# Softmax divisors moved from the probabilities to the attention outputs, with GpSimd issuing and multiplying

## The chip, the cores and the metric

The program runs on one core of a Trainium2 chip. The metric is the device time of one execution in microseconds; lower is better. The engines of the core work side by side, each through its own instructions in a fixed order: TensorE (PE, with its weight loads PEld), VectorE (DVE), ScalarE (ACT), GpSimd (POOL) and SyncE (SP, which here only issues transfers). An instruction that has to wait holds up everything behind it on its engine, and SP's queue of transfers behaves in the same way.

## The reference

One layer of a hybrid encoder on x[1024, 1024] in float32: RMSNorm, one input projection, three token mixers side by side (pooling, gated linear attention, forgetting attention), an output projection with residual, RMSNorm, a SwiGLU feed-forward part, a last RMSNorm. The change touches only the forgetting attention, eight heads of 64 channels:

```python
s = einsum('bhqd,bhkd->bhqk', qb, kh) + Fb[..., None] - F[:, :, None, :]
s = where(kpos[None, :] <= qpos[:, None], s, -inf)
p = softmax(s, axis=-1)                 # exp(s - max) / sum over the row
return einsum('bhqk,bhkd->bhqd', p, vh)
```

The division by a row's sum may stand on the probabilities or, since the product with V is linear, on the output of the row.

## The kernel before

Heads are worked in four pairs p = 0 to 3; a = 0 or 1 is the head in the pair. A head's 1024 queries are cut into eight blocks of 128; an item (a, m) holds two neighbouring blocks, qb = 2m and 2m + 1. `fox_item` does one item: for each block PE makes the scores (lines 575 to 578), DVE adds the forget term and finds the row's extreme (580), ACT takes the exponential and sums the row (584). Then DVE inverts the two sums (587), POOL multiplies the first block's probabilities by it (590) and DVE the second's (592). PE turns the probabilities over (601), ACT and DVE split each turned tile into a high and a low float32r half (603, 604), PE multiplies them with V (615), and ACT and DVE add the two halves of the output (618, 621). The output is laid with channels on partitions and queries along the free axis, so that in it a row's divisor lies along the free axis.

The outputs of pairs 0 to 2 gather in a tile Y and go through `keep_mix` (272 to 276): an ACT and a DVE pass, and two transfers to DRAM. Pair 3 writes its halves straight into `last_mix` (623 to 625).

The other work of this part of the program is projections that need no attention: Q and K of the next pair (`zq`, `zk`), V of pairs 2 and 3 (`psv`, from weights `wfv`), and, beside pairs 2 and 3, the output projection over channel tiles 0 to 3 (`pxa`) and then 4 to 7 (`pxb`, line 144, with weights `wo4` to `wo7`, each in a high and a low half). A scheduler of the framework orders each engine's instructions when the program is built; so an edit moves instructions far from its own lines.

Buffers come from numbered slots. Two rings matter. Ring `wr` has two slots; every raw projection weight passes through it: it is loaded by SP, split by ACT (high half, 118) and POOL (low half, 119), and only then may the slot's next user be written:

```python
RINGS = {"p": 6, "pp": 3, "fb": 2, "wr": 2, "w": 4}
def load_w(src, name, n=1024, eng=None):
    raw, (hi, lo) = R(f"{name}r", tag="wr"), (R(f"{name}{h}", F32R, tag="w") for h in "hl")
```

After pair 3 the slots of the rings `wr`, `w`, `p`, `pp` and `fb` join the common pool of slots (711, 712), in which the next tile takes the slot that was freed longest ago. Ring `fb` (two slots) holds the forget terms of the pair's two heads, broadcast by SP (631).

Of the kernel before, what the change touches and what calls it, by code (L numbers as in the profile page):

```python
# [18 lines left out]
P = 128  # L19
# [12 lines left out]
def tile_hybrid_block(ctx: ExitStack, tc, x, w_fv, w_gv, w_zt, w_o, w_gu, w_down, ln, w_pool, w_a3, chans, b_f, consts, out):  # L32
    nc = tc.nc
    ACT, DVE, POOL, PE, SP = nc.scalar, nc.vector, nc.gpsimd, nc.tensor, nc.sync
# [4 lines left out]
    dpool = ctx.enter_context(tc.tile_pool(name="dp", bufs=1, space=bass.MemoryType.DRAM))  # L39
# [10 lines left out]
    def G(name, dtype=F32):  # L50
        i = idle.pop(0)
        t_ = big.tile([P, 1024], dtype, tag=f"g{i}", name=name)
        where[name] = i
        return t_

    def free(*names):
        for n in names:
            idle.append(where.pop(n))

    def R(name, dtype=F32, tag="p"):  # L60

# [50 lines left out]
    def PS(tag, name):  # L112
        return pst.tile([P, 512], F32, tag=tag, name=name, bufs=BANKS[tag])
# [22 lines left out]
    def half(name, dtype=F32):  # L136
        return rng.tile([P, 512], dtype, tag="tmp", name=name, bufs=2)
# [25 lines left out]
    def names_T(name):  # L163
        return [f"{name}{k}_{c}_{h}" for k in range(4) for c in range(2) for h in range(2)]
# [127 lines left out]
    last_mix = []  # L292
# [253 lines left out]
                    POOL.tensor_copy(t_[a][own[1 - a], csl], f(t_[a][own[a], csl]))  # L546
        return Q, K, KL

    def fox_item(p, a, m, ops, fb, V, Y):

        Q, K, KL = (t_[a] for t_ in ops)
        nm = f"{p}_{a}_{m}"
        rows = slice(64 * a, 64 * a + 64)
        Pb, Ws = [], []
        l, rl = S(f"l{nm}", 2), S(f"rl{nm}", 2)
        for i in range(2):
            qb = 2 * m + i
            W = P * (qb + 1)
            nh = 1 if W <= 512 else 2
            w = W // nh  # L560
            qs = slice(qb * P, (qb + 1) * P)
            mn = S(f"mn{nm}_{i}")
            if m >= 2:
                pb = R(f"pb{nm}_{i}")
            elif i == 0:
                pb2 = R(f"pb{nm}")
                pb = pb2[:, 0:512]
            else:
                pb = pb2[:, 512:1024]
            top = 3.0e38  # L570
            for h in range(nh):
                s = PS("s", f"s{nm}_{i}_{h}")
                ks = slice(h * w, (h + 1) * w)
                last = h == nh - 1
                PE.matmul(s[:, 0:w], Q[:, qs], K[:, ks], start=True, stop=False)  # L575
                PE.matmul(s[:, 0:w], Q[:, qs], KL[:, ks], start=False, stop=not last)  # L576
                if last:
                    PE.matmul(s[:, w - P:w], identr, maskr, start=False, stop=True)
                t_ = mn if last else S(f"mw{nm}_{i}")
                DVE.tensor_tensor_reduce(out=pb[:, ks], in0=s[:, 0:w], in1=fb[:, ks], scale=1.0, scalar=top,  # L580
                                         op0=ALU.add, op1=ALU.min, accum_out=t_)
                top = t_[:, 0:1]

            ACT.activation(pb[:, 0:W], pb[:, 0:W], AF.Exp, bias=mn[:, 0:1], scale=-1.0, accum_out=l[:, i:i + 1])
            Pb.append(pb)
            Ws.append(W)
        DVE.reciprocal(rl, l)  # L587
        for i, (pb, W) in enumerate(zip(Pb, Ws)):
            if i == 0:
                POOL.tensor_tensor(out=pb[:, 0:W], in0=pb[:, 0:W], in1=rl[:, 0:1].broadcast_to([P, W]), op=ALU.mult)  # L590
            else:
                DVE.tensor_scalar(out=pb[:, 0:W], in0=pb[:, 0:W], scalar1=rl[:, 1:2], scalar2=None, op0=ALU.mult)
        o = PS("o", f"o{nm}")
        for n in range(m + 1):
            pt = PS("pt", f"pt{nm}_{n}")
            pp = R(f"pp{nm}_{n}", F32R, tag="pp")
            cut = P if n == m else 0
            for b in range(2):
                for i in range(b if cut else 0, 2):
                    o0 = 256 * b + P * i - cut * b  # L600
                    PE.transpose(pt[:, o0:o0 + P], Pb[i][:, (2 * n + b) * P:(2 * n + b + 1) * P], ident)  # L601
            w = 512 - cut
            ACT.activation(pp[:, 0:w], pt[:, 0:w], AF.Copy)  # L603
            DVE.tensor_tensor(out=pp[:, 512:512 + w], in0=pt[:, 0:w], in1=f(pp[:, 0:w]), op=ALU.subtract)  # L604
            for b in range(2):
                kb = 2 * n + b
                o0 = cut * b
                v_ = V[p % 2][kb // 4][:, kb % 4, a]
                ph = pp[:, 256 * b:512 - o0] if b else pp[:, 0:256]
                pl = pp[:, 768:1024 - o0] if b else pp[:, 512:768]  # L610
                both = (o[:, o0:256], v_.rearrange("p s e -> p (s e)"), ph)
                high = (o[0:64, o0:256], v_[:, 0], pl)
                last = kb == 2 * m + 1
                for n_, args in enumerate((high, both) if last else (both, high)):
                    PE.matmul(*args, start=(kb == 0 and n_ == 0), stop=(last and n_ == 1))  # L615
        tmp = half(f"ot{nm}")
        ot, oy = tmp[0:64, 0:256], tmp[:, 256:512]
        ACT.activation(ot, o[64:128, 0:256], AF.Copy)
        if p < 3:
            oy = Y[:, m * 256:(m + 1) * 256]  # L620
        DVE.tensor_tensor(out=oy[rows], in0=o[0:64, 0:256], in1=ot, op=ALU.add)
        if p == 3:
            hi, lo = (last_mix[m // 2][rows, h, (m % 2) * 256:(m % 2 + 1) * 256] for h in range(2))
            ACT.activation(hi, oy[rows], AF.Copy)
            POOL.tensor_tensor(out=lo, in0=oy[rows], in1=f(hi), op=ALU.subtract)

    def fox_attend(p, ops, V, Y):
        fbs = []
        for a in range(2):
            fb = R(f"fb{p}_{a}", tag="fb")  # L630
            SP.dma_start(fb, Fd[2 * p + a:2 * p + a + 1, :].broadcast_to([P, T]))
            fbs.append(fb)
        for a, m in ([(a, m) for a in range(2) for m in range(4)] if p < 3 else [(a, m) for m in (1, 0, 3, 2) for a in range(2)]):
            fox_item(p, a, m, ops, fbs[a], V, Y)


    x3d = [dpool.tile([P, D], F32, name=f"x3d{tb}") for tb in range(NT)]
# [36 lines left out]
    V = fox_values(0, (B.within(1), o_[0][:1], o_[0][1:], o_[1][:1], o_[1][1:] + B.turned(0), B.turned(1), (), ()))  # L674
    for k in range(8):
        keep_wo(k)
    ops = fox_qk(0)
    free("gv0", "gv1", "attb0", "attb1")
    for p in range(4):
        if p == 3:  # L680
            last_mix += [G(f"mix7_{g}", F32R).rearrange("p (h t) -> p h t", h=2) for g in range(2)]
        Y = G(f"y{p}") if p < 3 else None
        fox_attend(p, ops, V, Y)
# [12 lines left out]


    ws = [fetch_wo(k) for k in range(4)]
# [284 lines left out]
    sums = {}  # L983
# [139 lines left out]
```

## Time and profile before

| | |
|---|---|
| median of three runs | 1176.26 us (1174.48 to 1177.74) |
| the profiled execution | 1175.42 us, with a span of 1173.7 us from first to last instruction, so 1.7 us lie around the span |
| granted TensorE clock, mean | 0.992 |
| PE, DVE, ACT, POOL busy | 97%, 71%, 46%, 29% of the span |
| the attention pairs with their projections | about 226 to 478 us |
| output projection and second norm, up to the feed-forward part | to about 545 us |

The page's PE row counts a pipelined matmul from its start to its modelled end, so that PE reads as full at nearly any density; where it matters the pitch from one start to the next is used. Names such as `psv` or `wo5l` are the program's tiles with numbers left out.

### The profile page before, as it was taken

To read this page: it belongs to the slowest core of one execution; us is meant where nothing else is said; L and a number is where in the kernel's file an instruction comes from. 1 tells how busy PE (TensorE), PEld (TensorE's weight loads), DVE (VectorE), ACT (ScalarE), POOL (GpSimd) and SP (SyncE) were. 2 spreads that over 40 slices of the span, in tenths; PEclk is the share of its full clock that TensorE was granted. 3 is DMA by queue.
4 is the path that set the end of the run, shared out by engine and by line. 5 is a ranking of instruction groups with operands and counts; after the bars stand their busy time and mean duration, and the time that the engine had idled before them with its cause. 6 is when DMAs were issued, how large, how long until landed. Compare 5 with 4: busy or idle time off the path is not lost.

```text
span 1173.7 us, 15953 instructions
## 1 busy us (share of the span) xinstructions
PE 1136.0 (97%) x5928; PEld 958.5 (82%) x5928; DVE 828.2 (71%) x1365; ACT 536.0 (46%) x970; POOL 340.4 (29%) x260
## 2 busy tenths in 40 slices
PE   6999998999999999998999999999999999999996
PEld 5877878889978888886888888888888888888875
DVE  6697364387746866579997767767686685876686
ACT  6454233466654644456453433444344344334345
POOL 2231123343322413210302221022201370660784
PEclk9999999999999999999999999999999999999999
DMA  7121184411203734431323332242314688333233
GB/s 250 37 73 52 59 295 174 176 39 35 91 18 126 305 132 159 173 112 46 117 86 129 101 115 88 101 134 82 135 54 152 224 322 293 103 95 102 86 112 143
DMA packets 57692, 150.45 MB, mean 128 GB/s; under 512 B 5080, under 2 KB 5512, under 8 KB 57616
## 3 DMA queue, kind: packets, MB, share of 16 engines
q1 hardware_dynamic: 57184, 147.87, 36.5%
q0 software_dynamic: 432, 1.57, 0.4%
q8 instruction: 46, 0.75, 0.3%
q14 instruction: 30, 0.25, 0.1%
HBM read 105.09 MB, written 44.34 MB: 127 GB/s over the span
## 4 chain that ended last, share of the span: by engine, by line
PE 76%; DVE 4%; DMA 1%; issue 1%; POOL 1%; ACT 1%; SPq 0%; POOLq 0%; DVEq 0%; ACTq 0%
PE m L774 36%; PE d L1030 15%; PE pxa L144 4%; PE pxb L144 3%; PE o L615 3%; PE pt L601 2%; PE psv L152 2%; PE s L575 1%; PE s L576 1%; PE zq3p L152 1%; PE zq0p L152 1%; PE zq2p L152 1%; PE zk1p L152 1%; PE zk2p L152 1%; PE zk0p L152 1%
## 5 line engine op out<-in xcount | busy, mean ns | idle before, releaser
L774 PE MATMUL m<-hA_0h,wr 128*128 128x512 f32 x616 | 214.7, 391 | 1.2 <-ACT hr L729 1.2
L774 PE MATMUL m<-hA_1h,wr 128*128 128x512 f32 x616 | 214.9, 389 | 0.0
L774 PEld LDWEIGHTS m<-hA_0h,wr 128*128 128x128 f32 x616 | 116.1, 189 | 25.8 <-ACT hr L729 1.6
L774 PEld LDWEIGHTS m<-hA_1h,wr 128*128 128x128 f32 x616 | 115.8, 188 | 24.2
L1030 PE MATMUL d<-lw,ha 128*128 128x512 f32 x308 | 119.9, 389 | 0.9 <-DVE lw L880 0.9
L774 PE MATMUL m<-hA_0l,wr 128*128 128x512 f32 x308 | 120.3, 391 | 0.0
L774 PE MATMUL m<-hA_1l,wr 128*128 128x512 f32 x308 | 119.9, 389 | 0.0
L1030 PE MATMUL d<-hw,ha 128*128 128x512 f32 x308 | 119.3, 389 | 0.0
L1030 PE MATMUL d<-hw,la 128*128 128x512 f32 x308 | 118.4, 389 | 0.0
L756 ACT ACTIVATE wr<-ws 128x512 fp32r<-128x512 f32 x110 | 69.5, 632 | 101.5 <-DVE ws L755 50.1
L826 POOL TENSOR_TENSOR cg<-cu,cu 128x512 f32<-128x512 f32 x11 | 19.7, 1795 | 302.8 <-DVE cu L803 266.7
L757 DVE TENSOR_TENSOR wr<-ws,wr 128x512 fp32r<-128x512 f32 x110 | 76.8, 704 | 20.6 <-ACT wr L756 20.5
L880 DVE TENSOR_TENSOR la<-ra,ha 128x1024 fp32r<-128x1024 f32 (+1 forms) x42 | 57.2, 1368 | 32.0 <-ACT ha L879 24.7
L590 POOL TENSOR_TENSOR pb<-pb,rl 128x128 f32<-128x128 f32 (+3 forms) x32 | 39.0, 1222 | 117.5 <-DVE rl L587 108.9
L872 POOL TENSOR_TENSOR rw<-wd,wd 128x512 f32<-128x512 f32 x33 | 59.0, 1815 | 47.7 <-PE d L1030 47.6
L879 ACT ACTIVATE ha<-ra 128x1024 fp32r<-128x1024 f32 (+1 forms) x42 | 41.3, 987 | 65.6 <-DMA ra<-cd 56.8
L1030 PEld LDWEIGHTS d<-lw,ha 128*128 128x128 f32 x308 | 57.8, 188 | 13.3 <-DVE lw L880 1.3
L604 DVE TENSOR_TENSOR pp<-pt,pp 128x512 fp32r<-128x512 f32 (+1 forms) x80 | 50.2, 631 | 25.7 <-ACT pp L603 25.3
L774 PEld LDWEIGHTS m<-hA_0l,wr 128*128 128x128 f32 x308 | 58.1, 189 | 12.0
L774 PEld LDWEIGHTS m<-hA_1l,wr 128*128 128x128 f32 x308 | 58.0, 188 | 12.0
L1030 PEld LDWEIGHTS d<-hw,la 128*128 128x128 f32 x308 | 57.8, 188 | 12.1
L1030 PEld LDWEIGHTS d<-hw,ha 128*128 128x128 f32 x308 | 57.8, 188 | 11.9
(398 smaller groups left out, 2690.6 us busy)
## 6 DMA issues: line engine op xcount, KB each, us to landing
ra<-cd SPq DMA_DIRECT2D x35, 512.0 KB, 3.9
wu<-in_w_gu_dram SPq DMA_DIRECT2D x22, 512.0 KB, 4.6
wg<-in_w_gu_dram SPq DMA_DIRECT2D x22, 512.0 KB, 3.7
wd<-in_w_down_dram SPq DMA_DIRECT2D x22, 512.0 KB, 6.4
mix<-mixs SPq DMA_DIRECT2D x14, 512.0 KB, 5.3
cd<-cg SPq DMA_DIRECT2D x11, 512.0 KB, 6.3
cd<-cs SPq DMA_DIRECT2D x11, 512.0 KB, 3.4
cd<-cu SPq DMA_DIRECT2D x11, 512.0 KB, 3.3
```

The source lines that it names most:

```text
L144: PE.matmul(ps, a, b, start=(n == 0), stop=(n == last))
L152: PE.matmul(ps, a, b, start=(i == 0 and n == 0), stop=(i == len(terms) - 1 and n == 2))
L590: POOL.tensor_tensor(out=pb[:, 0:W], in0=pb[:, 0:W], in1=rl[:, 0:1].broadcast_to([P, W]), op=ALU.mult)
L604: DVE.tensor_tensor(out=pp[:, 512:512 + w], in0=pt[:, 0:w], in1=f(pp[:, 0:w]), op=ALU.subtract)
L615: PE.matmul(*args, start=(kb == 0 and n_ == 0), stop=(last and n_ == 1))
L756: ACT.activation(hi, src, AF.Copy)
L757: DVE.tensor_tensor(out=lo, in0=src, in1=f(hi), op=ALU.subtract)
L774: PE.matmul(ps, a, b, start=(n == 0), stop=(n == 11))
L872: POOL.tensor_tensor(out=raw_[:, j * 512:j * 512 + 512], in0=wd[h0, j0 + j][:, e0, :], in1=wd[h1, j0 + j][:, e1, :], op=op)
L879: ACT.activation(hi[:, sl], src, AF.Copy)
L880: DVE.tensor_tensor(out=lo[:, sl], in0=src, in1=f(hi[:, sl]), op=ALU.subtract)
L1030: PE.matmul(banks[t], a[:, o], b[:, ns], start=(j0 + j == 0 and m == 0), stop=(j0 + j == NF // 2 - 1 and m == 2))
```

## The change

The probabilities stay undivided. ACT's row sums go into one tile of 16 columns a pair (`sums`), and a new function `divide(p, Y, sums, g)` handles one half g (512 queries) of both heads of a pair: DVE inverts eight columns of sums, PE turns them to 8 rows of 128, ACT copies them to SBUF, POOL issues one transfer of these 4 KB to DRAM and two that bring them back, each spread over the 64 partitions of a head, and POOL multiplies Y by them. The SBUF side of all this lives in a slot of ring `wr`. For pairs 0 to 2 both halves are divided after the next pair's Q and K projections have been written down; in pair 3, whose output now goes to a Y of its own, the first half after item (1, 0) and the second at the end, each followed by the split into `last_mix`.

```diff
-        l, rl = S(f"l{nm}", 2), S(f"rl{nm}", 2)
...
-            ACT.activation(pb[:, 0:W], pb[:, 0:W], AF.Exp, bias=mn[:, 0:1], scale=-1.0, accum_out=l[:, i:i + 1])
+            ACT.activation(pb[:, 0:W], pb[:, 0:W], AF.Exp, bias=mn[:, 0:1], scale=-1.0, accum_out=sums[:, col(a, qb)])
             Pb.append(pb)
-            Ws.append(W)
-        DVE.reciprocal(rl, l)
-        for i, (pb, W) in enumerate(zip(Pb, Ws)):
-            if i == 0:
-                POOL.tensor_tensor(out=pb[:, 0:W], in0=pb[:, 0:W], in1=rl[:, 0:1].broadcast_to([P, W]), op=ALU.mult)
-            else:
-                DVE.tensor_scalar(out=pb[:, 0:W], in0=pb[:, 0:W], scalar1=rl[:, 1:2], scalar2=None, op0=ALU.mult)
...
-        DVE.tensor_tensor(out=oy[rows], in0=o[0:64, 0:256], in1=ot, op=ALU.add)
+        DVE.tensor_tensor(out=Y[rows, m * 256:(m + 1) * 256], in0=o[0:64, 0:256], in1=ot, op=ALU.add)
+
+    Ld = dpool.tile([4, 2, 2, 512], F32, name="Ld")
+    def divide(p, Y, sums, g):
+        nm = f"{p}_{g}"
+        rw = R(f"rb{nm}", tag="wr")
+        rl, rt, rb, gs = S(f"rl{nm}", 8), rw[0:8, 512:640], rw[:, 0:512], slice(g * 512, g * 512 + 512)
+        DVE.reciprocal(rl, sums[:, 8 * g:8 * g + 8])
+        pt = PS("pt", f"ptl{nm}")
+        PE.transpose(pt[0:8, 0:P], rl, ident)
+        ACT.activation(rt, pt[0:8, 0:P], AF.Copy)
+        POOL.dma_start(Ld[p, g].rearrange("a (q t) -> (a q) t", t=P), rt)
+        for a in range(2):
+            POOL.dma_start(rb[64 * a:64 * a + 64, :], Ld[p, g, a:a + 1, :].broadcast_to([64, 512]))
+        POOL.tensor_tensor(out=Y[:, gs], in0=Y[:, gs], in1=rb, op=ALU.mult)
         if p == 3:
-            hi, lo = (last_mix[m // 2][rows, h, (m % 2) * 256:(m % 2 + 1) * 256] for h in range(2))
-            ACT.activation(hi, oy[rows], AF.Copy)
-            POOL.tensor_tensor(out=lo, in0=oy[rows], in1=f(hi), op=ALU.subtract)
+            ACT.activation(last_mix[g][:, 0], Y[:, gs], AF.Copy)
+            POOL.tensor_tensor(out=last_mix[g][:, 1], in0=Y[:, gs], in1=f(last_mix[g][:, 0]), op=ALU.subtract)
...
         for a, m in ([(a, m) for a in range(2) for m in range(4)] if p < 3 else [(a, m) for m in (1, 0, 3, 2) for a in range(2)]):
-            fox_item(p, a, m, ops, fbs[a], V, Y)
+            fox_item(p, a, m, ops, fbs[a], V, Y, sums)
+            if p == 3 and (a, m) == (1, 0):
+                divide(p, Y, sums, 0)
+        if p == 3:
+            divide(p, Y, sums, 1)
...
-        Y = G(f"y{p}") if p < 3 else None
+        Y = G(f"y{p}")
...
             free(*done)
+            for g in range(2):
+                divide(p, Y, sums, g)
             keep_mix(4 + p, Y)
-            free(f"y{p}")
+        free(f"y{p}")
```

The orders move in three places that the prediction speaks of. Line numbers of the changed program are its own: 593 is the turning of probabilities (601 before), 607 the product with V (615), 626 the turning of the divisors, 628 and 630 their transfers, 631 the multiplication, 640 the forget terms (631 before), 662 the loads of `mix` (647 before), 721 the loads of `xa` (704 before).

**SP, transfers between pairs 0 and 1.** `fb_0` and `fb_1` are the forget terms; the second `fb_0` in the changed order is that of pair 2; `wfv` are the raw weights of V for pairs 2 and 3. Before:

```order
L282 DMA wod<-wos7h 128x1024
L117 DMA wfv_0r<-in_w_fv_dram 128x1024
L283 DMA wod<-wos7l 128x1024
L117 DMA wfv_1r<-in_w_fv_dram 128x1024
L117 DMA zq2r<-in_w_zt_dram 128x1024
L631 DMA fb_0_2686<-Fd 128x1024
L117 DMA zk2r<-in_w_zt_dram 128x1024
```

Changed:

```order
L283 DMA wod<-wos7l 128x1024
L640 DMA fb_0_2668<-Fd 128x1024
L640 DMA fb_1_2670<-Fd 128x1024
L640 DMA fb_0_3517<-Fd 128x1024
L117 DMA wfv_0r<-in_w_fv_dram 128x1024
L117 DMA wfv_1r<-in_w_fv_dram 128x1024
L117 DMA zq2r<-in_w_zt_dram 128x1024
```

In ring `wr` the tiles follow each other as zq1, zk1, then the two divisor tiles of pair 0, then the two `wfv`. Before, the `wfv` follow zq1 and zk1 directly. So now each `wfv` load stands behind a multiplication of pair 0's `divide`, and on SP behind pair 2's first forget term.

**PE, the last scores of pair 1's first head.** Before (`psv_5` is the sixth of eight blocks of V):

```order
L152 MATMUL psv_5_3319<-wfv_1h,hT_1_1_100 128x256
L152 MATMUL psv_5_3319<-wfv_1h,hT_1_0_99 128x256
L152 MATMUL psv_5_3319<-wfv_1l,hT_1_0_99 128x256
L615 MATMUL o_1_3_2487<-pp_1_3_2_2513,v_1_1509 64x256
L615 MATMUL o_1_3_2487<-pp_1_3_3_2525,v_1_1509 128x256
L601 MATMUL pt_0_0_0_2711<-ident,pb_0_0_2693 128x128 x3
L575 MATMUL s_0_3_1_1_2864<-k_0_2540,q_0_2538 128x512
```

Changed:

```order
L593 MATMUL pt_1_3_3_2486<-ident,pb_1_3_1_2437 128x128 x2
L607 MATMUL o_1_3_2449<-pp_1_3_2_2475,v_1_1510 64x256
L626 MATMUL ptl_0_2645<-ident,rl_0_2643 8x128
L574 MATMUL s_0_3_1_1_2830<-k_0_2502,q_0_2500 128x512
L575 MATMUL s_0_3_1_1_2830<-kl_0_2504,q_0_2500 128x512
L577 MATMUL s_0_3_1_1_2830<-maskr,identr 128x128
L607 MATMUL o_1_3_2449<-pp_1_3_3_2487,v_1_1510 128x256
L626 MATMUL ptl_1_2655<-ident,rl_1_2653 8x128
```

Before, 143 of the 192 `psv` matmuls of pairs 2 and 3 had gone by when these scores came; now none has: 106 matmuls and 49 turnings of attention alone stand between the third key tile of pair 0's item (0, 3) and this place, and the first `psv` stands 58 matmuls and 30 turnings behind `ptl_0`.

**SP, the weights of the second half of the output projection.** Before:

```order
L647 DMA mix_1_5074<-mixs 128x2x512
L647 DMA mix_0_4962<-mixs 128x2x512
L647 DMA mix_0_4966<-mixs 128x2x512
L740 DMA wu_5199<-in_w_gu_dram 128x1024
L647 DMA mix_0_4964<-mixs 128x2x512
L289 DMA wo5l<-wod 128x1024
L289 DMA wo7l<-wod 128x1024
L289 DMA wo6h<-wod 128x1024
L289 DMA wo6l<-wod 128x1024
```

Changed:

```order
L662 DMA mix_1_4986<-mixs 128x2x512
L662 DMA mix_0_4878<-mixs 128x2x512
L662 DMA mix_1_4984<-mixs 128x2x512
L756 DMA wg_5112<-in_w_gu_dram 128x1024
L662 DMA mix_1_4988<-mixs 128x2x512
L721 DMA xa_4789<-in_x_dram 128x1024
L289 DMA wo5l<-wod 128x1024
L289 DMA wo7l<-wod 128x1024
L289 DMA wo6h<-wod 128x1024
L289 DMA wo6l<-wod 128x1024
```

The tile `mix_1_4988` now has the slot of pair 3's second divisor tile, and `xa_4789` the slot of pair 3's Y, which is read last by the subtraction that ends `divide(3, 1)`. Both stood clear of the attention's end before (their slots were those of `zk3` and of pair 2's Y). On PE, the last of pair 3's products with V stood 66 `pxb` matmuls into the second half of the output projection; now they stand 24 `pxa` matmuls ahead of its first one.

More of the change, by code (lines that the diff above doesn't have):

```diff
@@ L547, in fox_qk, with fox_item @@
         return Q, K, KL
-    def fox_item(p, a, m, ops, fb, V, Y):
+    def fox_item(p, a, m, ops, fb, V, Y, sums):
         Q, K, KL = (t_[a] for t_ in ops)
@@ L553, in fox_item @@
         rows = slice(64 * a, 64 * a + 64)
-        Pb, Ws = [], []
-        l, rl = S(f"l{nm}", 2), S(f"rl{nm}", 2)
+        Pb = []
         for i in range(2):
@@ L632, in fox_attend @@
             fbs.append(fb)
+        sums = S(f"l{p}", 16)
         for a, m in ([(a, m) for a in range(2) for m in range(4)] if p < 3 else [(a, m) for m in (1, 0, 3, 2) for a in range(2)]):
-            fox_item(p, a, m, ops, fbs[a], V, Y)
+            fox_item(p, a, m, ops, fbs[a], V, Y, sums)
[3 more added lines that the diff above has]
+            divide(p, Y, sums, 1)
+        return sums
     x3d = [dpool.tile([P, D], F32, name=f"x3d{tb}") for tb in range(NT)]
@@ L681, in tile_hybrid_block @@
             last_mix += [G(f"mix7_{g}", F32R).rearrange("p (h t) -> p h t", h=2) for g in range(2)]
-        Y = G(f"y{p}") if p < 3 else None
-        fox_attend(p, ops, V, Y)
+        Y = G(f"y{p}")
+        sums = fox_attend(p, ops, V, Y)
         done = [f"{n}{p}_{a}" for n in ("q", "k", "kl") for a in range(2)] + [f"v{p}_{i}" for i in range(2)]
```

8 lines of the change are left out of this document (4 added, 4 removed).

## The prediction

> **What bounds the kernel now.** First the head of the page and its chain of waits, then the busy times by stretch.
>
> ```profile
> span 1173.7 us, 15953 instructions
> PE 1136.0 (97%) x5928; PEld 958.5 (82%) x5928; DVE 828.2 (71%) x1365; ACT 536.0 (46%) x970; POOL 340.4 (29%) x260
> PE 76%; DVE 4%; DMA 1%; issue 1%; POOL 1%; ACT 1%; SPq 0%; POOLq 0%; DVEq 0%; ACTq 0%
> 250.00:275.00 25.00, 25.00 (x187) 23.70 (x185) 21.62 (x56) 17.09 (x39) 12.30 (x13) 1.00 0.13 43
> 345.00:360.00 15.00, 11.76 (x62) 9.50 (x61) 7.39 (x14) 5.33 (x10) 7.34 (x8) 0.89 0.21 81
> 460.00:480.00 20.00, 19.78 (x124) 17.21 (x122) 10.30 (x20) 6.86 (x14) 3.60 (x4) 1.00 0.53 185
> ```
>
> The stretch rows give PE, PEld, DVE, ACT, POOL busy, then the granted clock. PE sets the time; DVE, ACT and POOL, which the change relieves, are 4%, 1% and 1% of the chain. Attention costs little because projections fill PE while a probability tile goes through ACT and DVE. The one hole inside the attention is at 345 to 360: 3.24 us idle, and the clock at 0.89 there takes another 0.11 x 15 = 1.65 us. The chain and the timeline of that place show it:
>
> ```profile
> 339.88 3.88 PE zk2p L152 x17
> 349.67 0.98 PE L615 MATMUL o<-pp,v 128*64 128x256 f32 x7 [0.34 <-DVE pp L604]
> 350.69 1.28 DVE L544 TENSOR_TENSOR kl<-zk2p,k 64x512 fp32r<-64x512 f32 x2 [0.61 <-PE o L615]
> 353.19 0.79 PE L152 MATMUL zq3p<-hT,zq3h 128*128 128x512 f32 x2 [2.55 <-DVE kl L544]
> 333.88 0.60 PE L601 MATMUL pt<-ident,pb 128*128 128x128 f32 x4
> ```
>
> The next projection waits until DVE, busy with an item's tail, has emptied a bank. So at best some 5 us of the attention can be won. The rows also give PE's pitch: 3.88 / 17 = 0.228 us for 512 columns, 0.446 ns a column, and (0.60 - 0.27) / 3 = 0.11 us for a turning, 0.27 being the modelled length of one, x2 taking 0.38.
>
> **The change part by part.** Removed are these, all on engines that PE hardly waits for; the rest of an item stays:
>
> ```profile
> L590 POOL TENSOR_TENSOR pb<-pb,rl 128x128 f32<-128x128 f32 (+3 forms) x32 | 39.0, 1222 | 117.5 <-DVE rl L587 108.9 <-PE pt L601 8.3
> L592 DVE TENSOR_SCALAR pb<-pb,rl 128x256 f32<-128x256 f32 (+3 forms) x32 | 29.3, 915 | 0.9
> L587 DVE RECIPROCAL rl<-l 128x2 f32<-128x2 f32 x32 | 5.2, 162 | 10.1 <-ACT pb L584 10.0
> L580 DVE CUSTOM_DVE_ANT_0 pb<-s,fb 128x128 f32<-128x128 f32 (+3 forms) x64 | 33.5, 534 | 8.5 <-issue 4.7 <-PE pt L601 2.1 <-PE s L578 0.7
> L580 DVE CUSTOM_DVE_ANT_0 pb<-s,fb,mw 128x320 f32<-128x320 f32 (+3 forms) x32 | 20.6, 645 | 2.9 <-PE s L578 2.2
> L604 DVE TENSOR_TENSOR pp<-pt,pp 128x512 fp32r<-128x512 f32 (+1 forms) x80 | 50.2, 631 | 25.7 <-ACT pp L603 25.3
> L621 DVE TENSOR_TENSOR y<-o,ot 64x256 f32<-64x256 f32 x24 | 9.9, 413 | 10.8 <-ACT ot L618 10.5
> L872 POOL TENSOR_TENSOR rw<-wd,wd 128x512 f32<-128x512 f32 x33 | 59.0, 1815 | 47.7 <-PE d L1030 47.6
> ```
>
> That is 39.0 us of POOL and 29.3 + 5.2 us of DVE, off the path; what the path gains is the hole at 350, 3.24 + 1.65 = **-4.9 us**, if the new order leaves it out (bounds 0 and -4.9). There the changed order has the pair's Q and K projections run after attention, with an idle DVE. Added on PE are eight turnings, 8 x 0.11 = **+0.9**. POOL's eight multiplications (1.8 us each by the row of line 872) and its 24 issues are fewer microseconds than the 39.0 removed; their price is who waits behind them. ACT's copy of pair 2's Y waits for POOL some 10 us after the divisors' turning, and PE has 9 us of other work there: nothing, though it costs the excess if transfers are slow.
>
> *Pair 1 without filler (D).* Every raw weight needs a slot that the divisors now hold, so `wfv` comes later than it did, and the attention before it runs bare. From the third key tile of pair 0's item (0, 3) to the end of its item (1, 3), PE has 29,696 columns and 49 turnings: 13.2 + 5.4 = 18.6 us. DVE stands there with 21 reductions (mean 54.1 / 96 = 0.564), 13 splits of 0.631, 5 output sums of 0.413, one split of K (0.69) and a reciprocal: 11.8 + 8.2 + 2.1 + 0.7 + 0.2 = 23.0 us. So DVE bounds it: 4.4 us over. At its densest before, DVE was busy 21.62 of 25 us; at that density it needs 26.6, 8.0 over. Low end 2, if DVE enters ahead. I take **+5**, near the full-density end, since nothing here waits for projections.
>
> *The wait for V's weights (W).* The rows:
>
> ```profile
> 218.84 0.33 SPq L117 DMA_DIRECT2D wfv_0r<-in_w_fv_dram  x1
> wfv_0r<-in_w_fv_dram SPq DMA_DIRECT2D x2, 512.0 KB, 4.2
> wfv_1r<-in_w_fv_dram SPq DMA_DIRECT2D x2, 512.0 KB, 3.9
> cd<-cu SPq DMA_DIRECT2D x11, 256.0 KB, 2.1
> lnfb<-in_ln_dram POOLq DMA_DIRECT2D x1, 512.0 KB, 3.8
> ln2b<-in_ln_dram POOLq DMA_DIRECT2D x1, 512.0 KB, 6.8
> 466.13 0.65 POOL L714 DMA_DIRECT2D ln2b<-in_ln_dram  x1 [6.45 <-PE pxa L144]
> L118 ACT ACTIVATE wfv_0h<-wfv_0r 128x1024 fp32r<-128x1024 f32 x1 | 1.1, 1061 | 2.0 <-POOL pb L590 2.0
> 240.54 2.41 POOL L119 TENSOR_TENSOR wfv_0l<-wfv_0r,wfv_0h 128x1024 fp32r<-128x1024 f32 x1 [2.04 <-ACT wfv_0h L118]
> ```
>
> No row shows 4 KB out or 128 KB back on POOL's queue. From below it is the 2.1 us of the smallest transfers, from above POOL's own 6.8; I take 2.5 out and 3.0 back, nearer the small size. From ACT's copy of the divisors: out 2.5; the second read issued 0.65 later and landed at 6.15; multiplied at 7.95; `wfv_0r` landed at 12.2; split by ACT at 13.2. PE reaches it after 15,360 columns and 30 turnings, 10.2 us, which is at 9.9 from that copy: **3.3 us** of waiting. The low half: POOL's next reads, multiplication and split (7.95 + 3.65 + 1.8 + 2.4) end at 15.8, PE is there at 14.8: **1.0**; the second weight tile adds 0.1. W = **+4.4**. With 2.1 us each it is 2.8; with 6.8 each it is 16. While ACT waits for `wfv_0r`, pair 1's exponentials stand behind it, so attention cannot fill the hole.
>
> By the Trainium skill, page "DMA: Bandwidth & Descriptors", section "Anatomy of one DMA — SWDGE (gpsimd) path", a GpSimd-issued transfer takes about 2.0 us plus its bytes over 436 KB per us. That would be 2.0 out and 2.3 back, and the sum would fall by 1.2 us here and 1.2 below. The trace disagrees for 512 KB: the formula gives 3.2, the rows 3.8 and 6.8.
>
> *The weights of the output projection's second half (T).* The timeline at the place:
>
> ```profile
> 466.08 0.33 SPq L289 DMA_DIRECT2D wo5l<-wod  x1
> 467.00 0.36 SPq L289 DMA_DIRECT2D wo6h<-wod  x1
> 470.12 0.19 PEld L144 LDWEIGHTS pxb<-wo5l,mix 128*128 128x128 f32 x1 [0.22 <-DMA wo5l<-wod]
> 467.00 7.58 DMA wo6h<-wod
> 474.62 0.73 PE L144 MATMUL pxb<-wo6h,mix 128*128 128x512 f32 x2 [0.22 <-DMA wo6h<-wod]
> wo6l<-wod SPq DMA_DIRECT2D x1, 512.0 KB, 8.3
> ```
>
> Before, these loads are on the chain already, hidden by attention of pair 3 between `pxb`. Now attention is over, and on SP they stand behind two transfers into slots that `divide(3, 1)` frees last. From ACT's last probability copy: divisor copy 0.3, out 2.8, back 6.45, multiplied 8.25, ACT's split 8.9, POOL's subtraction 10.7, `xa` issued 11.2, `wo5l` landed 4.0 later at 15.2. PE by then: DVE split and four products 1.0, 28 matmuls 6.4, so 7.4; it waits **7.8**. `wo6h`, issued 0.92 after `wo5l`, lands at 19.7 (7.58), PE is there at 17.0: **2.7**; `wo6l` (8.3) **0.8**. Less the 0.5 waited before, T = **+10.8**. Without any hold by POOL the same landings alone give 4.5; with 6.8 us transfers 19.
>
> *Clock.* The 0.89 above followed a hole of some 3 us. Two new holes of that size, each partly spent waiting anyway: **+1** (0 to 3.3).
>
> Sum: 5 + 4.4 + 10.8 + 0.9 + 1 - 4.9 = +17.2. The profiled execution's 1175.4 becomes 1192.6; the median of the runs stands 0.8 above it, so **1193 us**.
>
> **The rivals.**
>
> *Only the loads' own latency counts (D 2, W 0, T 4.5):* 1176.3 + 2 + 4.5 + 0.9 - 4.9 = 1179. For it: PE may reach these places later than its own work says, since ACT and DVE lag. Against: the divisors' transfers start behind the same ACT.
>
> *Faster.* The hole at 350 goes and nothing replaces it: 1176.3 - 4.9 + 0.9 = 1172. It decides where D, W and T together stay under 4 us. For it: each item's path from exponential to turning is shorter by a reciprocal and a POOL pass of 1.2 us. Against: 4.5 us of load latency without attention to cover it.
>
> *Slow transfers on POOL,* as `ln2b`: 1176.3 + 5 + 16 + 19 + 0.9 + 1 - 4.9 = 1213. For it: each divisor goes out and comes back before anything follows. Against: 4 KB and 128 KB are small.
>
> **How the numbers follow.** Forecast 0.67, loads alone 0.15, faster 0.08, slow transfers 0.10. Three runs tell about 0.3%, 3.5 us, from no change. Loads alone, at 1179, lies close to that bound: 0.06 of its 0.15 goes to no change and 0.09 to slower. So slower 0.67 + 0.10 + 0.09 = 0.86, same 0.06, faster 0.08. The forecast's own range by its bounds is 1184 to 1205; reaching to 1180 and 1207 takes in most of the loads-alone case and some of the slow one.
>
> **What would show it.** D: in pair 1 the stretches show DVE at 85% or more with PE pitch over 0.446 ns a column. W: `psv` waits for `wfv_0h` or `wfv_0l` for 3 us or more, and ACT at line 118 for the load. T: `pxb` waits for `wo5l` for 5 us or more with SP held at `xa`. Gain: no wait of a Q projection for a split of K. Wrong: POOL's transfers landing near 2 us with PE behind its own work, or another wait in pairs 2 and 3 of this size.

## The result

The changed kernel takes 1218.1 us (median of four runs, 1214.6 to 1218.9), the kernel before 1176.4 beside it: a ratio of 1.0343, with a 95% interval of 1.0327 to 1.0358. It is 41.7 us slower; the forecast was 17 us slower, with a range that ended at 1207. The head of the page of the changed kernel, and its chain of waits by engine:

```profile
span 1212.8 us, 15900 instructions
PE 1145.6 (94%) x5936; PEld 963.0 (79%) x5936; DVE 798.8 (66%) x1309; ACT 534.2 (44%) x972; POOL 321.5 (27%) x254
...
PE 69%; issue 4%; DVE 4%; DMA 3%; ACT 2%; POOL 2%; POOLq 0%; SPq 0%; DVEq 0%; ACTq 0%
```

DVE is 29 us less busy than before and POOL 19, as the change means; yet PE's share of the chain falls from 76% to 69%. The span is 39.1 us longer. Two groups of PE's products come after the same work in both kernels and so tell where the time went: the projection of Q for pair 3 (`zq3p`) and the last product of the output projection (`pxb`). The view of one tile gives each group's first and last start. Before:

```profile
L152 PEld LDWEIGHTS zq3p<-hT,zq3h x32: 186/188/331, 353.2 to 367.5; 128*128 128x128 f32 x32
L144 PE MATMUL pxb<-wo4h,mix x32: 389/391/481, 469.2 to 528.8; 128*128 128x512 f32 x32
```

After:

```profile
L152 PEld LDWEIGHTS zq3p<-hT,zq3h x32: 187/188/188, 359.1 to 371.8; 128*128 128x128 f32 x32
L144 PE MATMUL pxb<-wo4h,mix x32: 389/389/497, 508.1 to 566.5; 128*128 128x512 f32 x32
```

By the end of `zq3p`, with the attention of pairs 0 and 1 done, the changed kernel is 371.8 - 367.5 = 4.3 us behind. By the end of `pxb` it is 566.5 - 528.8 = 37.7 behind. So 33.4 us are lost in pairs 2 and 3 and the output projection, where the forecast had 10.8 and the clock. The stretches of the changed kernel show the places (columns as in the prediction: the stretch, then PE, PEld, DVE, ACT, POOL busy, granted clock, DMA share, GB/s):

```profile
250.00:275.00 25.00, 24.31 (x160) 21.38 (x159) 20.27 (x61) 20.11 (x47) 4.91 (x8) 1.00 0.12 43
275.00:300.00 25.00, 21.01 (x139) 17.56 (x139) 16.26 (x45) 17.09 (x40) 8.13 (x9) 0.92 0.28 79
440.00:475.00 35.00, 30.81 (x171) 26.75 (x170) 18.70 (x47) 15.82 (x32) 7.72 (x9) 0.90 0.50 174
475.00:520.00 45.00, 24.43 (x116) 18.48 (x115) 11.01 (x19) 6.14 (x13) 4.74 (x6) 0.77 0.37 123
```

The last of these stretches in the kernel before:

```profile
475.00:520.00 45.00, 45.00 (x242) 38.15 (x241) 30.29 (x40) 24.26 (x52) 9.17 (x14) 1.00 0.36 130
```

In the last stretch PE is busy for little over half of the time. The chain of waits there, from the turning of the last divisors to PE's next product, is the longest loss of the program (start, length, what; some links are left out at "..."):

```profile
484.22 0.12 PE ptl L626
484.37 0.28 ACT rb L627
...
484.93 2.66 DMA Ld<-rb
...
487.88 0.56 POOL rb L630
488.44 3.55 DMA rb<-Ld
...
492.12 1.26 POOL y L631
...
494.11 1.27 POOL mix L634
495.40 4.64 DMA xa<-in_x_dram
...
500.13 0.70 DVE xa L673
...
500.88 5.35 PE pxa L144 x15
```

Pair 3's second division goes out to DRAM, comes back, is multiplied and split; with POOL's last subtraction a slot comes free, into which SP loads a tile of x; DVE adds it to a finished sum; and only this frees the bank that PE needs. PE's own row, and DVE's, give the wait:

```profile
500.88 0.80 PE L144 MATMUL pxa<-wo0h,mix 128*128 128x512 f32 x1 [16.03 <-DVE xa L673]
500.13 1.29 DVE L673 TENSOR_TENSOR xa<-pxa,xa 128x512 f32<-128x512 f32 x2 [14.41 <-DMA xa<-in_x_dram]
```

Earlier, in pair 3, PE waits 3.53 us for `o`'s bank, which DVE empties late. ACT and DVE stand behind pair 2's `keep_mix`, which waits for POOL's product:

```profile
450.76 1.44 PE L607 MATMUL o<-pp,v 128*128 128x256 f32 x5 [3.53 <-DVE y L610]
448.07 1.06 ACT L273 ACTIVATE mh<-y 128x1024 fp32r<-128x1024 f32 x1 [2.85 <-POOL y L631]
449.16 1.23 DVE L274 TENSOR_TENSOR y<-y,mh 128x1024 f32<-128x1024 f32 x1 [2.60 <-ACT mh L273]
```

**Whose slot.** Following the allocator through the program (a tile takes the slot that was freed longest ago) gives the hand-ons. In the kernel before, x's seventh tile (`xa6`) takes the slot of pair 2's Y, free long before. In the changed kernel pair 3 has a Y too, and `xa6` takes that one's slot, which POOL reads to the end of the second division. On SP the loads of `wo5` to `wo7` stand behind `xa6`. Both banks for `pxa` hold `xa6`'s sums, so the 24 products of `xa7` can't start either. And `wo5l` has, in both kernels, the slot of a tile of `mix` that `xa7`'s products read; so its load can't leave before 15 of these 24 have run. The trace agrees: it was issued 10.8 us after `xa` (495.40), right behind the fifteenth:

```profile
505.82 0.39 PE L144 MATMUL pxa<-wo0h,mix 128*128 128x512 f32 x1
506.24 0.33 SPq L289 DMA_DIRECT2D wo5l<-wod  x1
```

### The profile page after: what moved, and what is told of

The parts are those of the page before. It is cut to its first block, busy times and chain, and to the rows that moved or that the text cites. A ratio compares the mean times of both kernels' runs of the same rounds, so it can differ in the third digit from the quotient of the medians.

```text
span 1212.8 us, 15900 instructions
## 1 busy us (share of the span) xinstructions
PE 1145.6 (94%) x5936; PEld 963.0 (79%) x5936; DVE 798.8 (66%) x1309; ACT 534.2 (44%) x972; POOL 321.5 (27%) x254
## 4 chain that ended last, share of the span: by engine, by line
PE 69%; issue 4%; DVE 4%; DMA 3%; ACT 2%; POOL 2%; POOLq 0%; SPq 0%; DVEq 0%; ACTq 0%
PE m L791 34%; PE d L1047 15%; PE pxa L144 3%; PE psv L152 2%; PE o L607 2%; PE pt L593 2%; PE pxb L144 2%; PE s L574 1%; PE s L575 1%; PE zk1p L152 1%; PE zk3p L152 1%; PE zq0p L152 1%; PE zk0p L152 1%; PE zq3p L152 1%; PE zq1p L152 1%
## 5 line engine op out<-in xcount | busy, mean ns | idle before, releaser
L897 DVE TENSOR_TENSOR lw<-rw,hw 128x1024 fp32r<-128x1024 f32 (+1 forms) x30 | 49.9, 1674 | 21.7 <-ACT hw L896 21.5
```

The source lines that it names most:

```text
L897: DVE.tensor_tensor(out=lo[:, sl], in0=src, in1=f(hi[:, sl]), op=ALU.subtract)
```

## The experiments

Two theories. **Slots:** the time is lost because tiles now live in slots that later transfers wait for (pair 3's Y, and the divisors in ring `wr`); the division itself is cheap, and the passes that it replaces were free. **Chain:** the division's own way (out to DRAM, back, GpSimd's product) delays what follows, wherever its tiles lie. Times are medians; ratios are to the kernel before, run beside them.

### Pair 3's Y kept

```diff
-        free(f"y{p}")
+            free(f"y{p}")
...
-    free(*[f"wo{k}{h}" for k in range(4) for h in "hl"], *done)
+    free(*[f"wo{k}{h}" for k in range(4) for h in "hl"], *done, "y3")
```

The first edit moves the line under `if p < 3`: only the Y of pairs 0 to 2 is handed on there.

> Pair 3's Y keeps its slot until the projections pxa are done, so no load of x needs that slot; everything else as in the change. Theory A (the 24 us that PE lost between 480 and 520 hang on the slot: x's last tile is loaded only when divide(3, 1) has ended): the 16 us wait before pxa and most of the waits on wo5l and wo6h go, 1218 - 22 to 24 = 1194 to 1197, with pxa and pxb between the last items. Rival B (they hang on the division itself, since the last projections need pair 3's divided output whatever slots are free): PE waits about as long, now before the first pxb that needs mix7, and the time stays within 5 us of 1218.

1191.0 us, ratio 1.0128 (1.0111 to 1.0145): 27 us of the 42 are gone, with every division where it was. The same stretch of this kernel:

```profile
475.00:520.00 45.00, 43.56 (x241) 36.70 (x240) 23.45 (x35) 17.21 (x40) 7.72 (x14) 1.00 0.56 193
```

PE is busy 43.56 of 45 us instead of 24.43. The chain of transfers is still there (pair 3's second one is issued at 496.29), but now PE has products beside it.

### The divisors out of the weights' ring

```diff
-        rw = R(f"rb{nm}", tag="wr")
...
+            rp = G(f"rb{p}")
             for g in range(2):
-                divide(p, Y, sums, g)
+                divide(p, Y, sums, g, rp)
+            free(f"rb{p}")
```

Each pair's divisors get one slot of the common store. Pair 3's (not shown) is taken before its first item and handed on, as its Y is, with the second division.

> The divisors get one slot a pair outside the ring of the raw weights; Y's slot is handed on as in the change. Theory A (that ring kept V's weights out of pair 1's attention, which cost 12 us between 250 and 320): psv stands between pair 1's items again, DVE-bound stretches and the wait on wfv_0h go, 1218 - 12 = 1206; the 16 us wait before pxa stays. Rival B (pair 1's dense stretch is slow because DVE is, filler or not): the loss moves into the other items and the time stays at 1214 to 1220.

1202.4 us, ratio 1.0228 (1.0205 to 1.0251): 15.7 us less. V's projection is back between pair 1's items. Its stretches, and PE's rows with a wait at the two places spoken of:

```profile
275.00:300.00 25.00, 25.00 (x207) 24.70 (x206) 13.71 (x43) 13.50 (x35) 1.14 (x2) 1.00 0.06 23
340.00:355.00 15.00, 11.41 (x76) 9.41 (x75) 7.62 (x13) 7.66 (x15) 7.80 (x11) 1.00 0.04 11
```

```profile
352.21 0.74 PE L152 MATMUL zq3p<-hT,zq3h 128*128 128x512 f32 x2 [2.44 <-DVE kl L544]
480.82 0.79 PE L144 MATMUL pxa<-wo0h,mix 128*128 128x512 f32 x1 [12.72 <-DVE xa L675]
```

The loss at 275 to 300 is gone; but the hole at 350 of the kernel before is back, with the divisions all on the output. So what took the hole away in the changed kernel was not the shorter items. It was V's late weights: `zq2`, `zk2` and `zq3` then ran in a row after pair 1. Two later runs with pair 3 as before say the same: no hole with the divisors in the ring, a hole again with them out of it. The wait before `pxa` is still 12.72 us, since x's slot was left as in the change.

### Both edits, and the divisors' slot of pair 3 kept too

```diff
+            rp = G(f"rb{p}")
...
-    free(*[f"wo{k}{h}" for k in range(4) for h in "hl"], *done)
+    free(*[f"wo{k}{h}" for k in range(4) for h in "hl"], *done, "y3", "rb3")
```

> Both edits: the divisors' slot apart from the ring, and neither pair 3's Y nor its divisors' slot handed on before pxa is done. Theory A, if the two are apart: 1218 - 23 - 12 = 1183, of which 9 us are the wait at 447 for pair 2's division (ACT and DVE held behind the copy of Y). Rival B (the chain of transfers on GpSimd itself delays work wherever the slots lie): 1200 or more, with new waits of 5 us or more on y, mh or mix.

1186.4 us, ratio 1.0085 (1.0066 to 1.0105). The wait of 3.53 us behind pair 2's copy went as well, which was not expected to: it was not the chain's alone. What is left, beside the hole at 350 (2.4 us of wait), stands at the beginning of `pxb`:

```profile
474.51 0.50 PE L144 MATMUL pxb<-wo4l,mix 128*128 128x512 f32 x1 [1.21 <-DMA wo4l<-wod]
485.57 0.77 PE L144 MATMUL pxb<-wo6h,mix 128*128 128x512 f32 x1 [3.35 <-DMA mix<-mixs]
```

### No division at all

```diff
-        rw = R(f"rb{nm}", tag="wr")
...
-        DVE.reciprocal(rl, sums[:, 8 * g:8 * g + 8])
...
-        POOL.tensor_tensor(out=Y[:, gs], in0=Y[:, gs], in1=rb, op=ALU.mult)
```

> The divisors and the multiplication are left out altogether (reciprocals, turnings, transfers, products); slots and order rules as in the change, so the output is not divided. Theory A (slots and the chain behind the division cost the time, and the removed passes over the probabilities won only the 5 to 7 us of the hole at 350): no wait at 290 and 447; Y's slot still goes to x but is free some 9 us earlier, so 5 to 8 us of the wait before pxa stay: 1218 - 12 - 9 - 10 = 1187. Rival B (all the loss is the division's chain): 1176 - 7 = 1169.

1198.8 us, ratio 1.0189 (1.0174 to 1.0205). This is the strongest evidence against the chain: with nothing to divide, and none of the passes over the probabilities, the kernel is still 23 us slower than before. The divisors' tiles leave ring `wr` with the division, so of the slots only that of pair 3's Y is as in the change. The time was expected to be lower (1187): the wait before `pxa` halves, but the waits on `wo5l` (1.1 us) and `wo6h` (2.3) behind it stay, and the hole at 350 is back.

```profile
482.97 0.80 PE L144 MATMUL pxa<-wo0h,mix 128*128 128x512 f32 x1 [8.15 <-DVE xa L664]
```

### The kernel before, with only a Y for pair 3

```diff
-        if p < 3:
+        if True:
             oy = Y[:, m * 256:(m + 1) * 256]
...
-        Y = G(f"y{p}") if p < 3 else None
+        Y = G(f"y{p}")
...
-            free(f"y{p}")
+        free(f"y{p}")
```

> The kernel before, probabilities divided as ever, with one edit: pair 3's sums go into a Y of their own (as pair 0's to 2's do), whose slot is handed on when its last item ends. Theory A (the slot's hand-on alone, not the division, costs the end of the attention): an x tile lands after the last item, PE waits 6 to 10 us before pxa and again on wo5l and wo6h, as without any division: 1176 + 20 = 1196 (1191 to 1200). Rival B (only GpSimd's division chain makes the slot late enough to matter): 1176 to 1180.

1200.8 us, ratio 1.0205 (1.0186 to 1.0225). This kernel divides its probabilities as ever; one tile more costs 24 us. Rows of SP, DVE and PE at the place:

```profile
477.04 0.36 SPq L704 DMA_DIRECT2D xa<-in_x_dram  x1
...
482.64 1.29 DVE L658 TENSOR_TENSOR xa<-pxa,xa 128x512 f32<-128x512 f32 x2 [6.89 <-DMA xa<-in_x_dram]
483.38 0.80 PE L144 MATMUL pxa<-wo0h,mix 128*128 128x512 f32 x1 [8.50 <-DVE xa L658]
```

The mechanism is that of the changed kernel, with 8.5 us of wait where the division's chain, which holds the slot longer, makes it 16. Here too the waits on `wo5l` (1.1 us) and `wo6h` (2.4) follow.

### Pairs 0 to 2 alone on the output

```diff
+        if p == 3:
...
-        Y = G(f"y{p}")
+        Y = G(f"y{p}") if p < 3 else None
```

Under `if p == 3` stand the reciprocal and the products on the probabilities, as in the kernel before, and pair 3 calls `divide` no more.

> The change for pairs 0 to 2 alone (divisors in the raw weights' ring, transfers and product on GpSimd); pair 3 divides its probabilities and needs no Y, as before. Theory A: the end of the attention is as before; the 12 us at 250 to 320 and the wait for pair 2's division (about 6) stay, and the hole at 350 stays away (7): 1176 + 12 + 6 - 7 = 1187. Rival B (the ring costs little and the end was all): 1176 to 1180.

1184.1 us, ratio 1.0067 (1.0050 to 1.0085), 3 us below the forecast; the wait behind pair 2's copy, put at about 6 there, is absent. The ring `wr` and the chain for three pairs cost 7.5 us, net of the hole that goes.

The next run adds the edit of the second experiment (`rp = G(...)` in place of the slot of ring `wr`) for pairs 0 to 2.

> As the run with pair 3 left as before, but the divisors of pairs 0 to 2 in a slot of their own outside the weights' ring. Theory A (nothing but slots cost time, and the removed passes won nothing by themselves): V's weights come early again, the hole at 350 is back, 1176 to 1180. Rival B (the relief of DVE and GpSimd is worth something once no slot is in the way): 1172 or less. Rival C (GpSimd's chain still delays pair 2's copy of Y): 1182 or more.

1179.6 us, ratio 1.0029 (1.0017 to 1.0042). So the ring is worth 4.5 of the 7.5, net. The hole at 350 is back (PE waits 2.4 us for `kl` there). The chain of transfers for pairs 0 to 2, one slot more in use, and all the relief of DVE and GpSimd there, together come to +3 us.

In its place, the next one spreads the divisors without transfers:

```diff
-        POOL.dma_start(Ld[p, g].rearrange("a (q t) -> (a q) t", t=P), rt)
...
+            ACT.activation(rx[:, :, a], rl[:, 4 * a:4 * a + 4].unsqueeze(2).broadcast_to([P, 4, 64]), AF.Copy)
...
+            PE.transpose(pt[:, q * P:(q + 1) * P], rx[:, q], ident)
+        DVE.tensor_tensor(out=Y[:, gs], in0=Y[:, gs], in1=pt, op=ALU.mult)
```

> As the run with pair 3 left as before, but the divisors of pairs 0 to 2 are spread over the rows by TensorE (ACT writes them out 64 wide, four turnings a half, DVE multiplies from the bank) and no transfer is left. 24 turnings of 0.1 us in place of 6: +2 on PE. Theory A (transfers cost nothing once slots are free): 2 above the run with the divisors' own slot, 1178 to 1181. Rival B (the transfers' 10 us chain was what delayed pair 2's Y and what follows): 4 or more below it.

1181.8 us, ratio 1.0053 (1.0035 to 1.0071): 2 us above the run before, as expected, though the two intervals overlap. Nothing is won by dropping the transfers; GpSimd's transfers were not what cost time there. This kernel needs no slot for divisors, so the store hands its slots on as in the kernel before, and it is still 5 us slower than that one. Some 2 of them were put down to the turnings; the rest is not explained by any slot.

### Two more slots

If slots are what runs out, more of them should help the kernel before as well. The hole at 350 looks like one: K's low halves of pair 2 (`kl2`) take the slots of V of pair 1, which pair 1's last products still read. Two slots of the probabilities' ring go to the common store, in four kernels:

```diff
-NSLOT = 33
+NSLOT = 35
-RINGS = {"p": 6, "pp": 3, "fb": 2, "wr": 2, "w": 4}
+RINGS = {"p": 4, "pp": 3, "fb": 2, "wr": 2, "w": 4}
```

> The kernel before with two more slots in the shared store, taken from the probabilities' ring (four in place of six); no division moved. Theory A (the hole of PE at 350 is a slot's hand-on: K's low halves of pair 2 lie where pair 1's last items still read V): the next projections fill pair 1's last items and the hole's 5 to 7 us go, 1169 to 1172, if four probability slots hold two items well enough. Rival B (the hole is DVE's order, late with the split): the hole stays, 1175 or more.

The kernel before with it: 1172.7 us, ratio 0.9963 (0.9949 to 0.9976), faster by 0.4%. `kl2` now lies in slots that are long free, and the hole is shut:

```profile
345.00:360.00 15.00, 15.00 (x90) 13.20 (x89) 9.18 (x22) 7.32 (x18) 3.91 (x4) 1.00 0.05 19
```

> The changed kernel with the same two slots moved from the probabilities' ring to the shared store. Theory A (at the end of the attention the store is what runs out, since pair 3's Y takes one slot and the last x tile waits for it): the last x tile gets an earlier slot and the 16 us wait goes; the loads of wo5 to wo7 still come late and V's weights still wait for the divisors: 1218 - 16 to 20 = 1198 to 1202. Rival B (the wait hangs on the chain of transfers): within 5 us of 1218.

The changed kernel with it: 1197.9 us, ratio 1.0179 (1.0163 to 1.0195). The time came within a microsecond of the forecast, the mechanism did not: the long wait is still there. Two places further down the list, pair 3's Y now hands its slot to `wo4h`, and PE waits for that:

```profile
496.49 0.80 PE L144 MATMUL pxb<-wo4h,mix 128*128 128x512 f32 x1 [15.83 <-DMA wo4h<-wod]
```

The 20 us were won around it: no wait behind pair 2's copy, and no wait on `wo5` and `wo6`.

> Outputs divided for pairs 0 to 2 with the divisors in a slot of their own, pair 3 as before, and the two slots moved from the probabilities' ring. Theory A (relief of DVE and GpSimd is worth nothing on its own, slots are): like the kernel before with two more slots, within 3 us, 1169 to 1174. Rival B (with the hole gone, shorter items let PE run through): 3 us or more below that kernel.

Pairs 0 to 2 on the output, divisors in their own slots, two more slots: 1171.7 us, ratio 0.9957 (0.9943 to 0.9971). That is 1 us below the kernel before with the same slots, and the two intervals overlap: with the hole shut, the relief of DVE and GpSimd is still not seen.

> The kernel before with two more shared slots, one from the probabilities' ring (five) and one from the ring of their transposed halves (two in place of three). Theory A: the hole at 350 goes as with four and three, 1169 to 1172, less what two transposed tiles in place of three cost in dense stretches. Rival B: the third transposed tile is what keeps PE fed, 1180 or more.

The slots taken in another way, one from the probabilities (`"p": 5`) and one from the transposed tiles (`"pp": 2`): 1184.1 us, ratio 1.0070 (1.0050 to 1.0091), slower. The hole at 350 is shut here too, and the store hands on the same slots as with four and three; so the 11 us between the two kernels come from the rings alone. PE's new waits are not in the dense stretches but on late loads of `mix`, 3.1 us before `pxa` and 6.4 in four waits before `pxb`; that the third transposed tile is what counts was not isolated.

> All four pairs divided on the output, divisors in slots of their own, pair 3's Y and divisors not handed on before pxa is done, and two slots moved from the probabilities' ring to the store: it differs from the earlier run with two more slots only in pair 3. Theory A (pair 3's own division costs 7 us only because its two slots are missing for the loads of mix and wo): 1172 to 1175. Rival B (its chain of transfers, 10 us with no attention left beside it, is what costs): 7 us or more above that run, 1178 to 1183.

All four pairs on the output, the divisors in their own slots, Y and divisors of pair 3 kept until `pxa` is done, and two more slots: 1172.2 us, ratio 0.9960 (0.9945 to 0.9974). It is faster than before by 0.4%, and 46 us faster than the changed kernel with the same divisions. It is level with the run that leaves pair 3's division as before (1171.7), and with the kernel before with two more slots (1172.7). Its stretches, and GpSimd's rows of pair 3's second division:

```profile
340.00:355.00 15.00, 15.00 (x92) 13.43 (x91) 7.97 (x22) 8.29 (x19) 4.77 (x5) 1.00 0.00 0
475.00:520.00 45.00, 45.00 (x220) 37.62 (x219) 29.68 (x35) 22.43 (x46) 10.78 (x16) 1.00 0.37 134
```

```profile
471.21 0.51 POOL L628 DMA_DIRECT2D Ld<-rb  x1 [13.15 <-ACT rb L627]
...
483.45 1.49 POOL L634 TENSOR_TENSOR mix<-y,mix 128x512 fp32r<-128x512 f32 x1 [2.35 <-ACT mix L633]
```

From 471.2 to 484.9 the chain is even longer than in the changed kernel, and PE is fully busy from 475 to 520 all the same. So where no late transfer hangs on its slots, the chain of pair 3 costs nothing that these runs can show.

**What the runs add up to.** Of the 41.7 us, pair 3's Y alone makes 24 (in the kernel before), and the three other pairs with the ring 7.5: 31.6 together. The remaining 10 us appear only with both, as the division's chain holds Y's slot longer (a wait of 16.0 instead of 8.5 us) and as one shared slot fewer lets pair 3's items run with less to do beside them (the wait at 450, of which only the run with pair 3's Y kept has a part left, 2.5 us). That last link is read from the traces; no run isolates it.

## Why the prediction was wrong

**The direction and the two causes were named; the step that failed is T's account of what PE does meanwhile.** That the divisors' slots and pair 3's Y would hold up loads, and that the end of the attention would be the dearest place, came true. But the sum let PE work beside the chain, and PE stood still. The clock and the copy of pair 2's Y, put at +1 and at nothing, make up most of the rest.

**D and W (+5 and +4.4).** With the gain of -4.9 and some turnings the forecast has the kernel about 5 us behind at the end of `zq3p`. Measured there: 4.3. That they agree is in part luck: behind the wait on `wfv_0h` the clock stood at half from 296.5 to 302.8, with PE at work for 5.89 us, which costs about 3 us that the forecast did not count here. By difference, with the gain taken as -4.9, D is then nearer 3 than 5; this is an estimate, as no run measures D alone. The rows of W in the changed kernel, PE, ACT, SP and POOL, and the reads of the divisors issued about 284 (size in KB, median time to landing):

```profile
296.54 0.80 PE L152 MATMUL psv<-wfv_0h,hT 128*128 128x256 f32 x2 [2.82 <-ACT wfv_0h L118]
295.43 1.06 ACT L118 ACTIVATE wfv_0h<-wfv_0r 128x1024 fp32r<-128x1024 f32 x1 [5.00 <-DMA wfv_0r<-in_w_fv_dram]
290.45 0.33 SPq L117 DMA_DIRECT2D wfv_0r<-in_w_fv_dram  x1
289.15 1.28 POOL L631 TENSOR_TENSOR y<-y,rb 128x512 f32<-128x512 f32 x1 [4.06 <-DVE pp L596]
rb<-Ld POOLq DMA_DIRECT2D x2, 128.0 KB, 4.9
```

PE waited 2.82 us for `wfv_0h`, where 3.3 were worked out, and did not wait for `wfv_0l` (1.0 forecast). The load was issued as soon as the first product had read the divisors. Both sides of the step came later than forecast, by about as much, so that the difference came out. Counted from ACT's first copy of divisors (280.95), `wfv_0h` was split after 15.5 us, where 13.2 were worked out, and PE stood there after 12.8, where it was 9.9. The profile puts the product's wait down to DVE's split, which ended 0.1 us before it; but Y was complete at 284.57, and the two reads of the divisors, issued from 283.52 on, took 4.9 us to land, where 3.0 were taken. So the transfer by itself held the product until about 288.9. D: DVE is busy 20.27 of 25 us from 250 to 275 (81%) and 65% in the next 25 us, less than the 85% asked for; PE lost time there, but ACT, at 20.11 of 25 us in the first of them, was as full as DVE.

**The gain (-4.9).** The hole did go, but not by the forecast's reason:

```profile
345.00:360.00 15.00, 15.00 (x70) 12.46 (x69) 4.67 (x6) 5.77 (x9) 7.32 (x8) 1.00 0.48 165
```

The prediction put it down to a DVE that empties a bank late. The run with the divisors out of the ring has shorter items and an idler DVE and keeps the hole; the kernel before with two more slots loses it. DVE's split waited for pair 1's last product, as the row quoted in the prediction says (`0.61 <-PE o L615`), because it writes where V lies. So this gain and the loss at W are two sides of one thing, V's late weights, and with the slots as they were could not be had apart.

**T (+10.8): the step that failed.** Its chain was right: from ACT's copy of the divisors at 484.37 to the load of x at 495.40 are 11.0 us, where 11.2 were forecast (on the chain the transfers were slower, 2.66 and 3.55 us for 2.5 and 3.0, and the product faster, 1.26 for 1.8). Wrong was what PE does meanwhile: "28 matmuls 6.4, so 7.4". Of these, 24 are `pxa`, and they need a bank. Both banks held the finished sums of the very tile whose x was being loaded. The prediction saw that SP is held at `xa`, and followed only the queue behind it, to `wo5l`; it did not follow the tile itself, to DVE's addition, to the bank, to PE. Nor could `wo5l` be issued straight behind `xa`, as the 15.2 has it, since its slot is free only when 15 of those 24 products have read `mix`. So PE's work fell behind the wait instead of hiding it: 16.03 us before `pxa`, then only 1.14 for `wo5l` and 2.25 for `wo6h`:

```profile
510.29 0.50 PE L144 MATMUL pxb<-wo5l,mix 128*128 128x512 f32 x1 [1.14 <-DMA wo5l<-wod]
514.68 1.22 PE L144 MATMUL pxb<-wo6h,mix 128*128 128x512 f32 x2 [2.25 <-DMA wo6h<-wod]
```

That is 19.4 less the 0.5 of before, 18.9 for a term of 10.8. The bound of 19 that the forecast had for T belongs to transfers of 6.8 us each, which did not come; that it is near is chance.

**The copy of pair 2's Y (nothing forecast).** "ACT's copy of pair 2's Y waits for POOL some 10 us after the divisors' turning, and PE has 9 us of other work there: nothing, though it costs the excess if transfers are slow." They were slower there than the 2.5 and 3.0 taken: 4.3 and 5.2 us (medians from 430 to 449). Counted from the second turning (434.84), ACT could copy after 13.2 us, not 10. PE even had 12.4 us of other work, not 9; but it waits for more than the copy. Behind ACT's copy (1.06 us) stand DVE's subtraction (1.23) and only then the addition that empties `o`'s bank, done 15.9 us after the turning. These last steps the sentence left out: 3.53 us of wait.

**The clock (+1).** The stretches of the changed kernel in which the clock stood at half:

```profile
449.80:456.60 6.80, 5.84 (x24) 5.45 (x25) 5.11 (x15) 3.70 (x9) 0.55 (x1) 0.50 0.74 262
487.30:504.40 17.10, 3.52 (x8) 2.81 (x9) 1.29 (x2) 0.63 (x1) 3.59 (x4) 0.50 0.40 125
514.60:518.00 3.40, 3.29 (x7) 2.19 (x8) 0.00 (x0) 0.00 (x0) 0.00 (x0) 0.51 0.53 218
```

Half of the time that PE worked in them is (5.84 + 3.52 + 3.29) / 2 = 6.3 us, where 1 was forecast and 3.3 was the bound, with two new holes; here are three, beside the one behind the wait on `wfv_0h`, whose 3 us are in the 4.3 above. The Trainium skill, page "TensorE: Matmul & The Clock Gate", section "What's actually happening", gives about 3.4 us of sustained work until the clock is full again. The trace agrees behind the long wait: PE starts again at 500.88 and the clock is full at 504.40. Behind the wait of 3.53 us it took longer, from 450.76 to 456.60.

**The sum.** 18.9 - 10.8 = 8.1 from T, 3.5 from pair 2's copy, 6.3 - 1 = 5.3 from the clock: 17 of the 24.5 us by which the forecast was short. Of the rest, some 7.6 us, 2.7 are in no trace: the profiled execution of the changed kernel (1214.6) lies 3.5 us under its median, where the forecast added 0.8. Another 1.4 arise behind `pxb`, where PE waits 5.8 us for the second norm and not 3.5. What is left is in smaller waits and is not attributed. The rival of slow transfers came out near the time (1213) for another reason: transfers of 6.8 us each were not seen, and dropping them, for pairs 0 to 2, wins nothing.

**The signs.** D's did not show (DVE at 81%, not 85%). W's showed in part: ACT waited for the load, and PE for 2.82 us where 3 were asked for. T's did not: 1.14 us before `wo5l`, not 5. The gain's did. What showed clearly is the last one, for being wrong: other waits in pairs 2 and 3 of this size, 16.03 and 3.53 us.

## What to carry to other kernels

- A new tile is never only its own work. It takes a slot, and where slots are handed on in order, every later tile moves one place: ask for each late tile which load waits for the slot, and follow that load past its queue to the engine that adds it, to the bank that this frees, and to PE. Moving the last reader of a slot can cost more than the work that was moved: here 24 us for one tile of 4 KB a partition.
- Before a change that saves work on an engine off the path, price the buffers that it adds. What two more slots are worth depends on what hangs on the slots: 4 us in the kernel before, 20 in the changed kernel. With the divisors and pair 3's Y also kept out of the way, two kernels that divide alike stand 46 us apart.
- A hole that closes beside a hole that opens may be one event moved: test by undoing the one cause and see whether both come back.

## What the runs showed of the hardware

Transfers issued by GpSimd were slower than taken and spread widely. The view of transfers of the changed kernel, with size and median time from issue to landing, and the view of the tile with the extremes over both kinds:

```profile
Ld<-rb POOLq DMA_DIRECT2D x8, 4.0 KB, 3.0
rb<-Ld POOLq DMA_DIRECT2D x16, 128.0 KB, 3.8
...
DMA to landing us min/median/max: 1.7/3.7/6.5
```

The forecast had 2.5 and 3.0. By the formula of the Trainium skill, page "DMA: Bandwidth & Descriptors", section "Anatomy of one DMA — SWDGE (gpsimd) path", they would be 2.0 and 2.3, as an estimate; the trace disagrees, and the measurement decides. GpSimd's product of 128 x 512 took 1.26 to 1.29 us, against the 1.8 taken from line 872, which has the same shape.
